# Four residual turns on a two-layer decoder trunk: where they stand on the load queue, and the order of the cases in the second column half of the down projection

## The chip, the cores and the metric

One Trainium2 chip, one of its cores. The time is device microseconds of one launch; three runs of the kernel before took 2044.64 to 2046.02 us, median 2045.53. Engines have short names: PE (matmul; PEld its weight loads), DVE (vector), ACT (scalar), POOL (GpSimd), SP (no arithmetic; here it issues nearly all DMAs, in program order).

## The reference, cut to what matters

A trunk of two layers over 256 tokens of width 2048, in float32: a mixer (gMLP gating in layer 0, latent attention in layer 1, each beside cross-attention into 256 memory tokens), then a gated ConvFFN. The change touches only the ConvFFN of both layers.

```python
def conv_ffn(h, w_up, cw, cb, w_down):     # h (256, 2048), w_up (2048, 11264), w_down (5632, 2048)
    a = h @ w_up
    ap = jnp.pad(a, ((0, 0), (CONV_W - 1, 0), (0, 0)))
    c = sum(ap[:, k:k + S] * cw[k] for k in range(CONV_W)) + cb
    gate, val = c[..., :D_FF], c[..., D_FF:]
    return (jax.nn.silu(gate) * val) @ w_down
...
x = x + conv_ffn(rmsnorm(x, g_ffn[l]), w_ffn_up[l], conv_w[l], conv_b[l], w_ffn_down[l])
```

## The kernel before

**Splitting.** Float32 products are made of three products of rounded halves. Each weight tile of 128 x 1024 floats (512 KB) is loaded into one of four tiles `raw`, ACT copies it rounded into `whi` (four tiles), DVE subtracts to get `wlo` (five tiles), and PE multiplies whi and wlo with the halves of the activations. A `raw` tile is free for the next load when DVE has made wlo; a `whi` tile is free when PE has used it. So loads run about four chunks ahead of the split and the split four ahead of PE. All weight loads go through SP's queue, which takes its entries in order: an entry that waits holds all behind it.

**Up projection.** 5632 columns are taken in 11 groups of 512, in three parts of 4, 4 and 3 groups. A group is two *passes* of PE (`gemm_fm`, L167): first gate, then value columns. A pass reads 2048 rows as eight *chunks* of 256 rows x 512 columns; each chunk is 24 matmuls (16 with whi, L161 and L162, and 8 with wlo, L164). Passes of a part are counted 0 to 7. Work that is to happen beside a pass hangs on it as `hooks`, a table from the chunk's number to functions that are called behind that chunk's matmuls. A pass's results go through DVE and ACT (convolution, SiLU, product).

**Turn.** The residual stream stands channel by channel (`x`, tile xT) and is needed token by token (`xt`) for the down projection. `turn(r)` (L1420), r from 0 to 3, makes one DVE transpose of 128 x 1024 floats into a tile `xs` (L1423) and four DMAs from xs to xt (L1427, 128 KB each in pieces of 32 floats). There are two tiles xs. All four turns hang on pass 3 of the first part, on chunks 0, 2, 4 and 6.

**Down projection.** A part of 4 groups has 2048 rows of `w_ffn_down`, eight *cases* k of 2 x 128 rows, and its output of 2048 columns is made in two *column halves* of 1024 (`down_phase`, L819), one after the other, with the cases in an order written in `FF_FAST`. A *plain* case splits its two row blocks and takes 24 matmuls of 512 columns. A *fast* case (k in 2, 3, 4, 5, 6) uses Winograd's form of a 2 x 2 block product and takes 21: it needs row block 1 (y), two tiles of block sums called t24 and t13, and the left half of row block 0 (x), split in this order (`fast_pair`, L800). The sums are four DVE adds of 128 x 512. They are made in one of three ways:

- *early* (`early_sums`, hung on the last passes), for the first column half;
- *stored* (`stored_sums`, L757): in a pass named in `FF_PASSES`, SP loads the two row blocks into the two tiles xs behind chunk 0, DVE adds (L759) behind chunk 3, POOL stores both tiles to DRAM (L785) behind chunk 5; the down projection loads them back (L861), into xs, or for case 5 of the second half into two `raw` tiles (`FF_RAW`);
- *late* (`late_sums`, L793): the down projection adds in place, from the loaded rows into xs.

With `FF_AHEAD`, the stored ones are case 3 of the first column half and cases 2, 5 and 4 of the second. In the second half cases 3 and 6 are late. Row tiles come from `raw`, for every third case from the two tiles `gate` (L851).

**What sets the order.** A scheduler places the instructions on each engine by its own timeline; inside `down_phase`, loads, splits and late sums are chained in the order in which they are written (`behind`).

Of the kernel before, what the change touches and what calls it, by code (L numbers as in the profile page):

```python
# [16 lines left out]
P = 128  # L17
# [15 lines left out]
FF_GROUPS = (4, 4, 3)  # L33
FF_EARLY = {4: (2, 6, 5), 3: (1, 2)}
FF_AHEAD = {4: ((3, 0), (2, 1), (5, 1), (4, 1)), 3: ()}
FF_PASSES = (0, 1, 2, 5), (1, 2, 4, 5), ()
FF_RAW = ((5, 1),)
FF_FAST = {
    4: (((2, 3, 4, 6, 5), (0, 1, 5, 2, 7, 3, 6, 4)), ((2, 3, 4, 6, 5), (0, 2, 1, 5, 3, 7, 4, 6))),
    3: (((1, 2, 4), (0, 3, 1, 5, 2, 4)), ((), (0, 1, 2, 3, 4, 5))),  # L40
}

# [35 lines left out]
class Kernel:  # L78
# [740 lines left out]
    def down_phase(self, dn, col, order, fast, lhs, rhs, pool, fp, between, evict, finish, late=0, late_gains=None, hooks={}, sums={}, stored={}):  # L819
        mm = self.nc.tensor.matmul  # L820
        names = ("m1", "m5", "m6", "m7"), ("e00", "e01", "e10", "e11")
        acc = {n: self.psum() for group in (names[::-1] if fast else names[1:]) for n in group}
        left, right = slice(0, 512), slice(512, 1024)
        todo = {n: 0 for n in acc}
        for k in order:
            for n in ("m1", "m5", "m6", "m7", "e00", "e01", "e10") if k in fast else names[1]:
                todo[n] += 1 if k in fast else 2
        total = dict(todo)

        def three(n, x, w, out=None, ends=None):  # L830
            (xh, xl), (wh, wl) = x, w
            start, stop = (todo[n] == total[n], todo[n] == 1) if ends is None else ends
            todo[n] -= 1
            o = acc[n] if out is None else out
            mm(o, xh, wh, start=start, stop=False)  # L835
            mm(o, xh, wl, start=False, stop=False)  # L836
            mm(o, xl, wh, start=False, stop=stop)  # L837

        def plain(k, ws, tb, half, **kw):
            cols = (left, right)[half]  # L840
            for i, (wh, wl) in enumerate(ws):
                three(f"e{tb}{half}", lhs(2 * k + i, tb), (wh[:, cols], wl[:, cols]), **kw)

        kept = []
        last_fast = [k for k in order if k in fast][-1:]
        for n, k in enumerate(order):
            raws = []
            for i in range(2):
                if n % 3 == (2 if col else 1) and n > 1:
                    raw = self.tmp(fp, [P, 1024], "gate", 2)  # L850
                else:  # L851
                    raw = self.wp.tile([P, 1024], F32, tag="raw", name=self.uid("raw"), bufs=4)
                c = 512 if (k in sums or (k, col // 1024) in stored) and i == 0 else 1024
                self.behind(self.nc.sync.dma_start(out=raw[:, :c], in_=dn[(2 * k + i) * P : (2 * k + i + 1) * P, col : col + c]))
                raws.append(raw)
            blocks = sums.get(k)
            if (k, col // 1024) in stored:
                tag, where, bufs = ("raw", self.wp, 4) if (k, col // 1024) in FF_RAW else ("xs", pool, 2)
                blocks = [self.tmp(where, [P, 1024], tag, bufs) for _ in range(2)]
                for i in (1, 0):  # L860
                    self.behind(self.nc.sync.dma_start(out=blocks[i], in_=stored[k, col // 1024][:, i]))  # L861
            elif k in fast and blocks is None:
                blocks = self.late_sums(raws, pool)
            if late_gains is not None and 2 <= n:
                late_gains(n - 2)
            if k in fast:
                names7 = "e00", "e01", "e10", "m6", "m5", "m7", "m1"
                for name, q, w in zip(names7, (1, 6, 2, 5, 4, 3, 0), self.fast_pair(raws, blocks)):
                    three(name, rhs(k, q), w)
                if k in last_fast:  # L870
                    between([acc[m] for m in names[0]])
            else:
                ws = self.plain_pair(raws)
                if n < len(order) - late:
                    for tb in range(2):
                        for half in range(2):
                            plain(k, ws, tb, half)
                else:
                    kept.append((k, ws))
            for f in hooks.get(n, ()):  # L880
                f()
        if not late:
            for tb in range(2):
                for half in range(2):
                    evict(tb, half, acc[f"e{tb}{half}"])
            return
        ET = mybir.EngineType
        with self.tc.manual_schedule(engines={ET.PE, ET.DVE, ET.Activation}):
            for half in range(2):
                for k, ws in kept:  # L890
                    plain(k, ws, 0, half)
                evict(0, half, acc[f"e0{half}"])
            for k, ws in kept:
                plain(k, ws, 1, 0)
            evict(1, 0, acc["e10"], meanwhile=lambda: finish(0))
            for k, ws in kept[:-1]:
                plain(k, ws, 1, 1)
            k, ws = kept[-1]
            e, rest = acc["e11"], self.psum()
            for i, (wh, wl) in enumerate(ws):  # L900
                three("e11", lhs(2 * k + i, 1), (wh[:, 512:768], wl[:, 512:768]), out=e[:, :256], ends=(False, i == 1))
            evict(1, 1, e, 0)
            for i, (wh, wl) in enumerate(ws):
                three("e11", lhs(2 * k + i, 1), (wh[:, 768:], wl[:, 768:]), out=rest[:, 256:], ends=(i == 0, i == 1))
            evict(1, 1, rest, 1)
            finish(1)


    def ffn(self, l, to_tokens, tokens):
# [6 lines left out]
        with self.tc.tile_pool(name=self.uid("ff"), bufs=1) as fp:  # L916
            g0 = 0
            for part, ng in enumerate(FF_GROUPS):
# [3 lines left out]
                fast = phases[0][0]  # L922
                parts7, o = {}, 0
                for k in fast:
                    n = 896 if k in phases[1][0] else 1024
# [22 lines left out]
                dn = down[g0 * 512 : (g0 + ng) * 512]  # L948
# [4 lines left out]
                for g in range(g0, g0 + ng):  # L953
# [34 lines left out]
                    hooks_g, hooks_v = dict(first) if g == 0 else {}, {}  # L988
                    if g == g0 + ng - 1:
                        hooks_g = sum_hooks  # L990
                    if g == 1:
                        hooks_v = to_tokens
                    if g == g0 + ng - 1:
                        hooks_v = ahead_hooks
                    if part and g == g0:
                        hooks_g = tokens.deferred()
                    both = lambda a, n: {i: a.get(i, []) + b.get(i, []) for b in (store_hooks.get(n, {}),) for i in {*a, *b}}
                    hooks_g, hooks_v = both(hooks_g, 2 * (g - g0)), both(hooks_v, 2 * (g - g0) + 1)
                    self.gemm_fm(self.rows(up, g * 512, 512), ks, 4, lambda k: xhl[k], eg, hooks=hooks_g)
                    self.gemm_fm(self.rows(up, FF + g * 512, 512), ks, 4, lambda k: xhl[k], ev, hooks=hooks_v)  # L1000
                g0 += ng
# [397 lines left out]
class Tokens:  # L1399
# [14 lines left out]
        return self.pool, 1024  # L1414

    def ffn(self, l):
        turns = {2 * r: [lambda r=r: self.turn(r)] for r in range(4)}
        self.k.ffn(l, turns, self)

    def turn(self, r):  # L1420
# [196 lines left out]
```

## Time and profile before

| | |
|---|---|
| median of 3 runs | 2045.53 us |
| profiled execution, its time | 2044.32 us |
| its span, first to last instruction | 2042.6 us |
| PE busy | 2019.6 us (99%) |
| DVE busy | 1650.9 us (81%) |
| ACT busy | 1177.1 us (58%) |
| PE's waits for ACT in up passes (L161 for L122) | 9.2 us in 5 |
| PE's waits for ACT in down projections (L835 for L713) | 3.1 us in 4 |
| granted TensorE clock, mean | 0.998 |

The span is shorter than the profiled execution's time by what lies around it. A row of a timeline is start, length, engine, line, operation, tiles written and read, and in brackets the idle time ahead and what ended it. Lines such as L835 (first product of a down case) are lines of the kernel before.

### The profile page before, as it was taken

What the parts mean: (1) busy time and instruction counts of PE and PEld (TensorE: products, weight loads), DVE (VectorE), ACT (ScalarE), POOL (GpSimd) and SP (SyncE); (2) the same over time, 40 slices, a digit from 0 to 9 for tenths busy, and PEclk for the clock granted to TensorE, in tenths of its full rate; (3) what the DMA queues carried; (4) which work ended last, traced back from release to release, by engine and by line L of the source; (5) the groups of instructions that cost most, each with busy time, mean ns of one, the idle gap of its engine ahead of it and who ended that gap; (6) DMA issues with size and microseconds to landing.
All of it is one profiled execution on the core that took longest, in us unless ns stands there. A gap on an engine that the chain in (4) does not pass through costs nothing.

```text
span 2042.6 us, 38329 instructions
## 1 busy us (share of the span) xinstructions
PE 2019.6 (99%) x15112; PEld 1909.2 (93%) x15112; DVE 1650.9 (81%) x2501; ACT 1177.1 (58%) x1687; POOL 130.0 (6%) x201
## 2 busy tenths in 40 slices
PE   9999999999999999999999999998999999999998
PEld 8989999999979999799989999998988999889996
DVE  6866767878988888887888786777898978888787
ACT  6754744545665556555566575444566555665555
POOL 0000013100000000000002141400000000000000
PEclk9999999999999999999999999999999999999999
DMA  8776556889668786677555634688876878667764
GB/s 253 234 216 183 165 194 210 272 213 308 217 222 277 250 305 209 221 216 229 178 194 183 185 113 160 207 260 220 305 225 223 290 241 305 205 222 218 236 203 148
DMA packets 262665, 455.40 MB, mean 223 GB/s; under 512 B 73102, under 2 KB 80596, under 8 KB 262484
## 3 DMA queue, kind: packets, MB, share of 16 engines
q1 hardware_dynamic: 257684, 435.63, 67.6%
q0 software_dynamic: 4608, 16.78, 2.3%
q8 instruction: 118, 1.93, 0.4%
q14 instruction: 63, 0.52, 0.1%
q10 hardware_dynamic: 192, 0.54, 0.1%
HBM read 429.82 MB, written 18.87 MB: 220 GB/s over the span
## 4 chain that ended last, share of the span: by engine, by line
PE 86%; DMA 5%; DVE 5%; ACT 2%; issue 1%; SPq 1%; ACTq 0%; DVEq 0%
PE ps L161 19%; PE ps L162 19%; PE ps L164 19%; PE ps L836 6%; PE ps L835 6%; PE ps L837 6%; PE ps L193 2%; PE ps L194 2%; PE ps L195 2%; DMA raw<-in_w_ffn_up 2%; DMA raw<-in_w_ffn_down 1%; PE ps L528 1%; DVE wlo L123 1%; DMA xs<-in_w_ffn_down 1%; DMA stored<-xs 1%
## 5 line engine op out<-in xcount | busy, mean ns | idle before, releaser
L122 ACT ACTIVATE whi<-raw 128x1024 fp32r<-128x1024 f32 x484 | 511.5, 1060 | 484.8 <-PE ps L162 303.9
L161 PE MATMUL ps<-xhl,whi 128*128 128x256 f32 x3264 | 765.0, 277 | 9.2 <-ACT whi L122 9.2
L123 DVE TENSOR_TENSOR wlo<-raw,whi 128x1024 fp32r<-128x1024 f32 x484 | 598.7, 1241 | 208.8 <-ACT whi L122 207.1
L162 PE MATMUL ps<-xhl,whi 128*128 128x256 f32 x3264 | 762.8, 276 | 0.0
L161 PEld LDWEIGHTS ps<-xhl,whi 128*128 128x128 f32 x3264 | 613.3, 188 | 10.9 <-ACT whi L122 10.2
L162 PEld LDWEIGHTS ps<-xhl,whi 128*128 128x128 f32 x3264 | 613.5, 188 | 0.7
L164 PE MATMUL ps<-xhl,wlo 128*128 128x256 f32 x3264 | 437.5, 276 | 0.2 <-DVE wlo L123 0.2
L164 PEld LDWEIGHTS ps<-xhl,wlo 128*128 128x128 f32 x3264 | 401.2, 188 | 0.4 <-DVE wlo L123 0.4
L836 PE MATMUL ps<-wlo,h 128*128 128x512 f32 x388 | 151.1, 390 | 0.0
L714 DVE TENSOR_TENSOR wlo<-raw,whi 128x1024 fp32r<-128x1024 f32 x100 | 120.8, 1220 | 31.8 <-ACT whi L713 31.0
L713 ACT ACTIVATE whi<-raw 128x1024 fp32r<-128x1024 f32 x100 | 104.7, 1056 | 69.1 <-PE ps L162 26.5
L943 ACT ACTIVATE c<-a,cT 128x256 f32<-128x256 f32 x176 | 99.6, 592 | 57.5 <-DVE a L241 57.1
L837 PE MATMUL ps<-whi,h 128*128 128x512 f32 x340 | 132.3, 390 | 0.0
L835 PE MATMUL ps<-whi,h 128*128 128x512 f32 x388 | 125.7, 394 | 3.6 <-ACT whi L713 3.1
L161 PE MATMUL ps<-mainhl,whi 128*128 128x256 f32 x512 | 119.7, 277 | 0.0
L162 PE MATMUL ps<-mainhl,whi 128*128 128x256 f32 x512 | 119.3, 276 | 0.0
L713 ACT ACTIVATE whi<-xs 128x1024 fp32r<-128x1024 f32 x60 | 62.1, 1057 | 60.1 <-DVE xs L793 26.3
L162 PEld LDWEIGHTS ps<-mainhl,whi 128*128 128x128 f32 x512 | 96.0, 188 | 0.0
L161 PEld LDWEIGHTS ps<-mainhl,whi 128*128 128x128 f32 x512 | 95.9, 188 | 0.0
L835 PEld LDWEIGHTS ps<-whi,h 128*128 128x128 f32 x388 | 71.8, 188 | 22.9 <-ACT whi L713 8.7
L128 DVE SCALAR_TENSOR_TENSOR wlo<-raw,gT,whi 128x512 fp32r<-128x512 f32 x96 | 71.5, 782 | 22.9 <-ACT whi L127 22.8
L714 DVE TENSOR_TENSOR wlo<-xs,whi 128x1024 fp32r<-128x1024 f32 x60 | 72.1, 1222 | 18.7 <-ACT whi L713 17.5
(388 smaller groups left out, 3032.1 us busy)
## 6 DMA issues: line engine op xcount, KB each, us to landing
raw<-in_w_ffn_up SPq DMA_DIRECT2D x352, 512.0 KB, 4.8
raw<-in_w_ffn_down SPq DMA_DIRECT2D x102, 512.0 KB, 5.5
raw<-in_w_out SPq DMA_DIRECT2D x64, 512.0 KB, 4.2
raw<-in_w_in_a SPq DMA_DIRECT2D x56, 512.0 KB, 4.5
gate<-in_w_ffn_down SPq DMA_DIRECT2D x42, 512.0 KB, 5.2
stored<-xs POOLq DMA_DIRECT2D x32, 512.0 KB, 5.2
raw<-in_w_mem_kv SPq DMA_DIRECT2D x31, 512.0 KB, 4.7
xs<-stored SPq DMA_DIRECT2D x24, 512.0 KB, 4.8
```

The source lines that it names most:

```text
L122: nc.scalar.activation(hi[:, :n], raw[:, :n], AF.Copy)
L123: nc.vector.tensor_tensor(lo[:, :n], raw[:, :n], hi[:, :n].bitcast(F32), ALU.subtract)
L128: nc.vector.scalar_tensor_tensor(lo[:, s], raw[:, s], gains[k], hi[:, s].bitcast(F32), ALU.mult, ALU.subtract)
L161: mm(acc[:, :S], wh, x[:, :S], start=first, stop=False)
L162: mm(acc[:, :S], wh, x[:, S:], start=False, stop=False)
L164: mm(acc[:, :S], wl, x[:, :S], start=False, stop=last)
L713: self.behind(self.nc.scalar.activation(hi, w, AF.Copy))
L714: self.behind(self.nc.vector.tensor_tensor(lo, w, hi.bitcast(F32), ALU.subtract))
L835: mm(o, xh, wh, start=start, stop=False)
L836: mm(o, xh, wl, start=False, stop=False)
L837: mm(o, xl, wh, start=False, stop=stop)
L943: nc.scalar.activation(c, a, AF.Identity, scale=w(2), bias=w(3))
```

## The change

All four parts of the edit are in the FFN.

1. `FF_PASSES`, first part: the pairs of stored sums hang on passes 2, 3, 4, 5 where they hung on 0, 1, 2, 5.
2. The turns: turns 0 and 1 hang on chunks 1 and 5 of pass 0, turns 2 and 3 on chunks 1 and 5 of pass 1, of the first group alone.
3. Second column half, parts of four groups: the order of cases is 0, 2, 1, 3, 5, 4, 7, 6 where it was 0, 2, 1, 5, 3, 7, 4, 6. Row tiles at place 5 come from `gate`: case 4's now, case 7's before.
4. A case with stored sums loads row block 1, t24, t13 and then the left half of row block 0, as they are used; before, it loaded the half row block 0, row block 1, t24, t13.

```diff
-FF_PASSES = (0, 1, 2, 5), (1, 2, 4, 5), ()
+FF_PASSES = (2, 3, 4, 5), (1, 2, 4, 5), ()
...
-    4: (((2, 3, 4, 6, 5), (0, 1, 5, 2, 7, 3, 6, 4)), ((2, 3, 4, 6, 5), (0, 2, 1, 5, 3, 7, 4, 6))),
+    4: (((2, 3, 4, 6, 5), (0, 1, 5, 2, 7, 3, 6, 4)), ((2, 3, 4, 6, 5), (0, 2, 1, 3, 5, 4, 7, 6))),
...
-                c = 512 if (k in sums or (k, col // 1024) in stored) and i == 0 else 1024
-                self.behind(self.nc.sync.dma_start(out=raw[:, :c], in_=dn[(2 * k + i) * P : (2 * k + i + 1) * P, col : col + c]))
                 raws.append(raw)
+            kept_sums = stored.get((k, col // 1024))
+            load = lambda o, a: self.behind(self.nc.sync.dma_start(out=o, in_=a))
+            row = lambda i, c: load(raws[i][:, :c], dn[(2 * k + i) * P : (2 * k + i + 1) * P, col : col + c])
             blocks = sums.get(k)
-            if (k, col // 1024) in stored:
+            if kept_sums is None:
+                row(0, 1024 if blocks is None else 512)
+                row(1, 1024)
+            else:
                 tag, where, bufs = ("raw", self.wp, 4) if (k, col // 1024) in FF_RAW else ("xs", pool, 2)
                 blocks = [self.tmp(where, [P, 1024], tag, bufs) for _ in range(2)]
+                row(1, 1024)
                 for i in (1, 0):
-                    self.behind(self.nc.sync.dma_start(out=blocks[i], in_=stored[k, col // 1024][:, i]))
-            elif k in fast and blocks is None:
+                    load(blocks[i], kept_sums[:, i])
+                row(0, 512)
+            if k in fast and blocks is None:
                 blocks = self.late_sums(raws, pool)
...
-                    if g == 1:
-                        hooks_v = to_tokens
...
-                    both = lambda a, n: {i: a.get(i, []) + b.get(i, []) for b in (store_hooks.get(n, {}),) for i in {*a, *b}}
-                    hooks_g, hooks_v = both(hooks_g, 2 * (g - g0)), both(hooks_v, 2 * (g - g0) + 1)
+                    if g == 0:
+                        hooks_g, hooks_v = hooks_g | to_tokens[0], to_tokens[1]
+                    hooks_g, hooks_v = store_hooks.get(2 * (g - g0), hooks_g), store_hooks.get(2 * (g - g0) + 1, hooks_v)
...
-        turns = {2 * r: [lambda r=r: self.turn(r)] for r in range(4)}
+        turns = [{1 + 4 * i: [lambda r=2 * n + i: self.turn(r)] for i in range(2)} for n in range(2)]
```

**SP's queue, layer 0, the four turns, before** (pass 3 of the first part). A row is the line, the operation, the tile written with its numbers and what is read; `xt<-xs` x4 is a turn, `raw<-in_w_ffn_up` a chunk's load.

```order
L1427 DMA xt_4187<-xs_709_5110 32x32x32 x4
L112 DMA raw_724_5248<-in_w_ffn_up 128x2x512
L112 DMA raw_727_5278<-in_w_ffn_up 128x2x512
L1427 DMA xt_4187<-xs_716_5176 32x32x32 x4
L112 DMA raw_731_5314<-in_w_ffn_up 128x2x512
L112 DMA raw_749_5389<-in_w_ffn_up 128x2x512
L1427 DMA xt_4187<-xs_723_5242 32x32x32 x4
L112 DMA raw_752_5419<-in_w_ffn_up 128x2x512
L112 DMA raw_755_5449<-in_w_ffn_up 128x2x512
L1427 DMA xt_4187<-xs_730_5308 32x32x32 x4
```

**The same turns in the change**: the first row stands behind the load of pass 0's last chunk; raw_626 is pass 1's first chunk, raw_665 pass 2's first.

```order
L1432 DMA xt_4187<-xs_590_4268 32x32x32 x4
L112 DMA raw_626_4503<-in_w_ffn_up 128x2x512
L112 DMA raw_629_4533<-in_w_ffn_up 128x2x512
L1432 DMA xt_4187<-xs_607_4405 32x32x32 x4
L112 DMA raw_633_4569<-in_w_ffn_up 128x2x512
L112 DMA raw_636_4599<-in_w_ffn_up 128x2x512
L112 DMA raw_639_4629<-in_w_ffn_up 128x2x512
L112 DMA raw_642_4659<-in_w_ffn_up 128x2x512
L1432 DMA xt_4187<-xs_632_4563 32x32x32 x4
L112 DMA raw_646_4695<-in_w_ffn_up 128x2x512
L112 DMA raw_649_4725<-in_w_ffn_up 128x2x512
L112 DMA raw_665_4796<-in_w_ffn_up 128x2x512
```

and directly behind them, where xs_668 and xs_669 are the first pair's tiles for stored sums, the same two places that turns 2 and 3 use:

```order
L764 DMA xs_668_4826<-in_w_ffn_down 128x1024
L112 DMA raw_670_4831<-in_w_ffn_up 128x2x512
L1432 DMA xt_4187<-xs_645_4689 32x32x32 x4
L112 DMA raw_673_4861<-in_w_ffn_up 128x2x512
L112 DMA raw_676_4891<-in_w_ffn_up 128x2x512
L764 DMA xs_669_4827<-in_w_ffn_down 128x512 x2
```

Two loads stand between the first two turns as before, four between the second and third and between the third and fourth; the first pair of stored sums stands on both sides of the fourth turn. On DVE the first transpose now stands at the start of the FFN:

```order
L255 SCALAR_TENSOR_TENSOR xhl_466_3354<-xT_81,gT_76,xhl_466_3354 128x256
L1428 STREAM_TRANSPOSE xs_590_4268<-xT_81 128x1024
L255 SCALAR_TENSOR_TENSOR xhl_466_3354<-xT_81,gT_76,xhl_466_3354 128x256 x3
L123 TENSOR_TENSOR wlo_603_4347<-raw_601_4345,whi_602_4346 128x1024
L123 TENSOR_TENSOR wlo_606_4377<-raw_604_4375,whi_605_4376 128x1024
L1428 STREAM_TRANSPOSE xs_607_4405<-xT_81 128x1024
```

These were four L255 in one row before; L255 makes operands for the last chunks of pass 0.

**SP's queue, layer 0, first part, second column half, before**: the two blocks of case 5, the rows of cases 3 and 7, the half row, row and blocks of case 4, and the rows of case 6.

```order
L861 DMA raw_1009_6996<-stored_687_4985 128x1024
L861 DMA raw_1008_6995<-stored_687_4985 128x1024
L854 DMA raw_1017_7035<-in_w_ffn_down 128x1024
L854 DMA raw_1018_7037<-in_w_ffn_down 128x1024
L854 DMA gate_1028_7081<-in_w_ffn_down 128x1024
L854 DMA gate_1029_7083<-in_w_ffn_down 128x1024
L854 DMA raw_1034_7117<-in_w_ffn_down 128x512
L854 DMA raw_1035_7119<-in_w_ffn_down 128x1024
L861 DMA xs_1037_7122<-stored_805_5850 128x1024
L861 DMA xs_1036_7121<-stored_805_5850 128x1024
L854 DMA raw_1045_7161<-in_w_ffn_down 128x1024
L854 DMA raw_1046_7163<-in_w_ffn_down 128x1024
```

**The same place in the change**, with the semaphores that each entry waits for: rows of case 3; row 1, t24, t13 and half row 0 of case 5; the same four of case 4; rows of case 7. Case 6's rows are the next two. A DMA signals one of eight DMAHW semaphores in turn, and waits for its own last use and for the load that last filled its tile; DMAHW3 is that of case 3's row block 1 (raw_1007), DMAHW2 that of its row block 0 (raw_1006), DMAHW7, ahead of this piece, that of case 2's row block 0.

```order
L855 DMA raw_1006_6991<-in_w_ffn_down 128x1024 [waits DMAHW2_49,DVE_49]
L855 DMA raw_1007_6992<-in_w_ffn_down 128x1024 [waits DMAHW3_49,DVE_49]
L855 DMA raw_1018_7038<-in_w_ffn_down 128x1024 [waits DMAHW4_49,DVE_49]
L855 DMA raw_1020_7040<-stored_766_5566 128x1024 [waits DMAHW7_49,DMAHW5_49,DVE_49]
L855 DMA raw_1019_7039<-stored_766_5566 128x1024 [waits DMAHW6_49,DMAHW3_49,DVE_49]
L855 DMA raw_1017_7037<-in_w_ffn_down 128x512 [waits DMAHW2_49,DVE_49]
L855 DMA gate_1029_7082<-in_w_ffn_down 128x1024 [waits DMAHW0_49]
L855 DMA xs_1031_7084<-stored_805_5850 128x1024 [waits DMAHW1_49]
L855 DMA xs_1030_7083<-stored_805_5850 128x1024
L855 DMA gate_1028_7081<-in_w_ffn_down 128x512
L855 DMA raw_1039_7125<-in_w_ffn_down 128x1024 [waits DMAHW4_49,DVE_49]
L855 DMA raw_1040_7126<-in_w_ffn_down 128x1024 [waits DMAHW5_49,DVE_49]
```

Case 3 came ahead of case 5, case 4 stands directly behind case 5, and case 7 between 4 and 6; the half row of each stored case went from first to last.

## The prediction

> **What bounds the kernel now.** I read the page first: PE is busy for 99% of the span, so only its stalls can be won. The waits of PE, first over the whole span, then by stretches (360 to 480, 1320 to 1440, 550 to 650, 840 to 900, 1800 to 1850 us), give their places; columns are total us, times, longest.
>
> ```profile
> PE 2019.6 (99%) x15112; PEld 1909.2 (93%) x15112; DVE 1650.9 (81%) x2501; ACT 1177.1 (58%) x1687; POOL 130.0 (6%) x201
> ...
> PE ps L161 <- ACT whi L122: 9.2, 5, 3.0
> PE ps L835 <- ACT whi L713: 3.1, 4, 1.5
> ...
> PE ps L161 <- ACT whi L122: 3.7, 2, 3.0
> PE ps L161 <- ACT whi L122: 5.4, 3, 2.8
> PE ps L835 <- ACT whi L713: 0.9, 1, 0.9
> PE ps L835 <- ACT whi L713: 1.9, 2, 1.5
> PE ps L835 <- ACT whi L713: 0.3, 1, 0.3
> ```
>
> All 9.2 us of L161 lie in two places, the fourth pass of each layer's FFN, where the four turns stand. The L835 waits lie in second column halves. What is late in the fourth pass, by SP's timeline and then ACT's and PE's:
>
> ```profile
> 417.23 5.08 SPq L1427 DMA_DIRECT2D xt<-xs  x4
> 422.41 1.47 SPq L112 DMA_DIRECT2D raw<-in_w_ffn_up  x2
> ...
> 431.77 6.62 SPq L1427 DMA_DIRECT2D xt<-xs  x4
> 438.49 1.89 SPq L112 DMA_DIRECT2D raw<-in_w_ffn_up  x2
> 440.47 5.29 SPq L1427 DMA_DIRECT2D xt<-xs  x4
> 445.85 12.73 SPq L112 DMA_DIRECT2D raw<-in_w_ffn_up  x6
> ...
> 452.50 1.06 ACT L122 ACTIVATE whi<-raw 128x1024 fp32r<-128x1024 f32 x1 [5.56 <-DMA raw<-in_w_ffn_up]
> ...
> 453.61 0.39 PE L161 MATMUL ps<-xhl,whi 128*128 128x256 f32 x1 [3.00 <-ACT whi L122]
> ```
>
> Each turn holds the queue for 5.1 to 6.6 us, and only two weight loads get between two turns. From the first turn to the load at 445.85 that is 28.6 us for six loads. PE eats a chunk (24 matmuls) in 2.72 us, eight of them at 0.91 us by the chain row below, so it needed ten and a half. The load lands at 452.4, ACT splits it in 1.06, PE stands.
>
> ```profile
> 363.86 0.91 PE ps L164 x8
> 598.91 1.13 PE ps L835 x5
> ...
> 363.00:373.00 10.00, 10.00 (x88) 9.95 (x87) 8.00 (x10) 5.32 (x6) 0.00 (x0) 1.00 0.74 250
> 454.00:464.00 10.00, 10.00 (x76) 10.00 (x76) 10.00 (x20) 6.06 (x9) 0.00 (x0) 0.83 0.66 206
> ```
>
> The windows (length, busy us of PE, PEld, DVE, ACT, POOL, then the granted clock, DMA share, GB/s) show one more price: behind the 3.00 us stall the clock is 0.83 for 10 us, so 1.7 us are lost with PE "busy". Layer 1's stalls, 2.8 us at most, have no such row. The Trainium skill (TensorE: Matmul & The Clock Gate, What's actually happening) lets the clock fall to half only after an idle window of about 3.4 us, whose phase runs freely. By its length the 3.00 us stall would be too short and the term 0 instead of 1.7. The row decides, and the sum keeps 1.7.
>
> **The change part by part.**
>
> *Turns.* Sixteen issues per layer leave the fourth pass, with four DVE transposes of 1.24 us; two turns go into each pass of the first group. Removed if none of it returns: 3.7 + 5.4 us of waits and 1.7 us of clock, 10.8. Idle counts too late: a 256-column matmul is 0.28 us long in the row below, and the next starts 0.11 after it, so each stall holds 0.17 more, five times 0.17 = 0.8. Together 11.6 us.
>
> Does it return? The start of layer 0's FFN:
>
> ```profile
> 353.73 0.28 PE L161 MATMUL ps<-xhl,whi 128*128 128x256 f32 x1
> 353.84 0.28 PE L162 MATMUL ps<-xhl,whi 128*128 128x256 f32 x1
> ...
> 353.25 1.42 DVE L667 TENSOR_TENSOR xT<-ps,xT 128x256 f32<-128x256 f32 x4 [0.36 <-PE ps L164]
> 354.58 1.44 DVE L123 TENSOR_TENSOR wlo<-raw,whi 128x1024 fp32r<-128x1024 f32 x1
> 355.94 3.36 DVE L255 SCALAR_TENSOR_TENSOR xhl<-xT,gT,xhl 128x256 fp32r<-128x256 f32 x4
> ...
> L1423 DVE STREAM_TRANSPOSE xs<-xT 128x1024 f32<-128x1024 f32 x4 | 5.0, 1240 | 2.0 <-DMA xt<-xs 2.0
> L759 DVE TENSOR_TENSOR xs<-xs,xs 128x512 f32<-128x512 f32 x8 | 5.5, 688 | 3.1 <-DMA xs<-in_w_ffn_down 3.0
> ...
> xt<-xs SPq DMA_DIRECT2D x32, 128.0 KB, 6.3
> raw<-in_w_ffn_up SPq DMA_DIRECT2D x352, 512.0 KB, 4.8
> ```
>
> In the new order the first transpose stands behind one L255, so it ends near 356.8 + 1.24 = 358.1. The first turn's issues take 5.1 to 6.6 and end at 363.2 to 364.7; two loads follow at the pace of their split, then the second turn, to 370 to 373. The load behind it is pass 1's third chunk. Landing 4.8 (median) to 6.6 us later (the 445.85 load) and 1.06 for ACT give 376.1 to 380.9. PE starts at 353.7, so pass 1 at 353.7 + 8 x 2.72 = 375.5 and that chunk at 380.9. Slack 0 to 5 us. Four loads then pass before the third turn. The fourth turn is the other narrow place: behind it only two loads are ahead of xs_669, which needs that turn's landing (6.3 us), and SP waits. That turn's transpose stands behind the split of pass 1's sixth chunk, whose split tile PE frees with the second chunk, at 375.5 + 2 x 2.72 = 380.9; with the split (1.1 on ACT, 1.2 on DVE) and the transpose it is near 385, its issues end near 391, its pieces land near 397. Then xs_669 goes, and at 397.6 the next load, pass 2's fifth chunk, split by 397.6 + 5.5 + 1.1 = 404.2; PE wants it at 375.5 + 21.8 + 10.9 = 408.2. Slack 4. I take 0.5 us of new stall per layer, 0 to 5.5 as bounds (5.5 is layer 1's whole old cost), so 11.6 - 1.0 = 10.6.
>
> *Stored sums into passes 2 to 5.* Two pairs per layer move from passes 0 and 1: four adds of 0.69 and 1 MB in, 1 MB out each. Pass 3 loses 5.0 us of transposes and gains 2.7 of adds; the total on DVE and DMA is unchanged. What covers it, in windows of an old pass with a pair (397), with turns (419) and with a pair again (461):
>
> ```profile
> 397.00:419.00 22.00, 22.00 (x196) 22.00 (x195) 18.70 (x32) 11.58 (x17) 1.06 (x2) 1.00 0.89 296
> 419.00:441.00 22.00, 22.00 (x196) 22.00 (x195) 16.59 (x23) 9.70 (x14) 0.00 (x0) 1.00 0.92 183
> 461.00:483.00 22.00, 22.00 (x196) 22.00 (x195) 21.90 (x37) 13.20 (x18) 1.06 (x2) 1.00 0.91 301
> ```
>
> A pair runs beside a full PE. Cost 0, but DVE has 0.1 us left in the last of them; without this cover see the third rival.
>
> *Second halves, four of them per kernel.* The old stall before the last case, 6 (SP, then ACT, then PE):
>
> ```profile
> 597.11 1.46 SPq L861 DMA_DIRECT2D xs<-stored  x2
> 598.67 0.85 SPq L854 DMA_DIRECT2D raw<-in_w_ffn_down  x2
> ...
> 607.34 1.06 ACT L713 ACTIVATE whi<-raw 128x1024 fp32r<-128x1024 f32 x1 [0.95 <-DMA raw<-in_w_ffn_down]
> 610.97 2.01 ACT L713 ACTIVATE whi<-xs 128x1024 fp32r<-128x1024 f32 x2 [2.57 <-DVE xs L793]
> ...
> 612.08 0.73 PE L835 MATMUL ps<-whi,h 128*128 128x512 f32 x2 [0.93 <-ACT whi L713]
> ```
>
> Case 6's rows stand behind case 4's two blocks; the second, issued near 599.1, lands 8.1 us later, then four adds, then ACT, and PE waits 0.93. In the new order a plain case, 7, stands between 4 and 6. A matmul of 512 columns takes 0.227 us (1.13 for five), so a fast case 21 x 0.227 = 4.8 and a plain one 24 x 0.227 = 5.4. Case 6's rows now wait for case 5's tiles, freed one by one up to near 598, so they no longer leave as one burst, and its sums start when 7's splits are done, near 604.3; 604.3 + 2.7 + 1.1 = 608.1 against PE's 610.7. The old waits go: 3.1 + 4 x 0.16 (0.39 long, 0.227 apart) = 3.7 us.
>
> What is late next: case 5's blocks. They lie in raw tiles; the semaphores in the rows of the change show t24 in the tile of case 2's row 0, free at 581.5 as before, and t13 in the tile of case 3's row 1, free once case 1's split (583.30 + 1.23 below), the sums (2.7) and that row's split are done: 588.5. With 5.5 us for landing and 1.1 for ACT it is there at 595.1; PE, at 590.5 with case 3, wants it 29 matmuls later, at 597.1. Only then, behind case 3's row 0 at 591.5, do case 4's four loads leave, 1.75 MB close together with case 5's half row. With 6.5 us they are split 0.4 us before PE wants t24 of case 4 (600.5); with 8.1, 1.2 us too late. I take 0.3 per half, 0 to 1.2 as bounds: 3.7 - 1.2 = 2.5.
>
> ```profile
> 583.30 1.23 DVE L714 TENSOR_TENSOR wlo<-gate,whi 128x1024 fp32r<-128x1024 f32 x1 [0.37 <-ACT whi L713]
> ...
> raw<-in_w_ffn_down SPq DMA_DIRECT2D x102, 512.0 KB, 5.5
> ```
>
> *First halves.* Only the stored case 3 changes, its half row asked for last. PE shows no wait there; it is read last on PE too. Cost 0.
>
> Sum on the profiled span: 2042.6 - 10.6 - 2.5 = 2029.5. That execution took 2044.32, 1.7 beyond its span and 1.2 under the median of 2045.53, so as a median 2045.5 - 13.1 = **2032.4 us**.
>
> **The rivals.**
>
> *The turns' stall only moves.* For it: a turn's time is its small pieces, 92% DMA share at 183 GB/s in the 419 window against 89% at 296, and a slack of 0 at the slow end. Against: two turns a pass rather than four, and the two in front start with all loads ahead. Then only the clock and the second halves are won: 2045.5 - 1.7 - 2.5 = 2041.3. The Trainium skill (DMA: Bandwidth & Descriptors, Specifications) wants 512 bytes at least for line rate; the turn's pieces are 32 floats, 128 bytes. The rule speaks for this rival, since moving a turn makes no piece larger.
>
> *Second halves get worse.* If 8.1 us is the landing time of each burst, 1.2 us a half in t24 and about as much again in t13 behind it: 4 x 2.4 = 9.6 instead of 3.7 gone: 2045.5 - 10.6 - 3.7 + 9.6 = 2040.8; with half of it, 2036.
>
> *DVE becomes the bound, slower than before.* DVE works in order and stands at an add until its block lands: 3.1 us before eight adds (L759 row). In passes 2 to 5 it now meets four pairs in a row with 0.1 us spare. ACT and the loads are about 11 us ahead of PE (four split tiles of 2.72 us). If each pair costs DVE more than (11 + 8)/4 = 4.8 us of standing, a layer loses over 8 us, and two lose more than the 15 saved; at 5.5 us it is 2 x (22 - 11) = 22, so 2045.5 - 13.1 + 22 = 2054. Against: three pairs in a row ran in passes 0 to 2 without a PE wait.
>
> **How the numbers follow.** Forecast, both stalls mostly gone (2027 to 2036): 0.65. Second halves worse: 0.15. Turn stall moved: 0.11. DVE bound: 0.05. Another place, either sign: 0.04. If no stall replaces the old ones, 2045.5 - 15.3 = 2030; a few tenths of unlisted short waits put the low end at 2027. Upwards the range takes in the second rival: 2041. A measurement of this kernel tells about 0.2% (4 us) from no change: faster 0.86 (the forecast, the second rival, part of the first), same 0.08, slower 0.06.
>
> **What would show it.** Right: no wait of PE on L122 in the fourth pass of either layer, clock 1.00 behind it; turns in pairs on SP with four loads before the third; none or under 0.5 us of L835 waits in second halves. Wrong: PE waits in the second or third pass (third chunk, fifth chunk), a wait for case 4's or 5's blocks, or DVE at 22 of 22 with idle time "<-DMA xs" in passes 2 to 5.

## The result

The changed kernel took 2027.24 us (median of 5, 2025.17 to 2030.53) beside 2044.64 for the kernel before: a ratio of 0.9921, 95% interval 0.9906 to 0.9935, so 17.4 us less. A second comparison on another chip gave 0.9924 (0.9903 to 0.9944), 2027.65 beside 2042.88, so 15.2 us less; one of its four executions, at 2523.7 us, is left out of the ratio. The forecast was 2032.4, in a range of 2027 to 2036. Ahead of the second comparison, 12 to 15 us were expected if the two halves of the edit (below) simply add up and 16 to 19 if each makes room for the other; its interval, 11.4 to 19.8 us, decides nothing between them.

The page's engine line and the full list of PE's waits of the changed kernel, the span being 2023.5 us:

```profile
PE 2013.4 (100%) x15112; PEld 1907.3 (94%) x15112; DVE 1649.4 (82%) x2501; ACT 1181.3 (58%) x1687; POOL 128.2 (6%) x201
...
PE ps L495 <- DVE ones L292: 1.1, 1, 1.1
PE ps L836 <- DVE wlo L714: 0.2, 1, 0.2
PE ps L608 <- DVE pT L250: 0.2, 1, 0.2
```

Both groups of the prediction, L161 for L122 and L835 for L713, are gone, and what is left lies outside the change. SP's timeline shows the turns (L1432 now) in pairs with four loads before the third, and the windows (the columns as before) a full PE at clock 1.00 in the first two passes and where the stall with the slow clock had been:

```profile
358.30 4.12 SPq L1432 DMA_DIRECT2D xt<-xs  x4
362.51 1.50 SPq L112 DMA_DIRECT2D raw<-in_w_ffn_up  x2
364.22 5.97 SPq L1432 DMA_DIRECT2D xt<-xs  x4
370.30 2.86 SPq L112 DMA_DIRECT2D raw<-in_w_ffn_up  x4
373.78 7.37 SPq L1432 DMA_DIRECT2D xt<-xs  x4
...
353.00:375.00 22.00, 22.00 (x195) 21.95 (x194) 19.64 (x23) 10.74 (x13) 6.75 (x8) 1.00 0.79 186
375.00:397.00 22.00, 22.00 (x197) 22.00 (x196) 15.28 (x21) 12.98 (x17) 0.00 (x0) 1.00 0.96 243
440.00:465.00 25.00, 25.00 (x223) 25.00 (x222) 21.21 (x36) 12.26 (x14) 1.06 (x2) 1.00 0.80 276
```

In the second half, ACT's rows for case 5's two blocks, then case 4's first block:

```profile
586.58 1.07 ACT L713 ACTIVATE whi<-raw 128x1024 fp32r<-128x1024 f32 x1 [0.70 <-PE ps L837]
587.94 1.06 ACT L713 ACTIVATE whi<-raw 128x1024 fp32r<-128x1024 f32 x1 [0.29 <-PE ps L837]
...
593.38 1.06 ACT L713 ACTIVATE whi<-xs 128x1024 fp32r<-128x1024 f32 x1 [0.72 <-DMA xs<-stored]
```

Case 5's blocks lie ready and ACT waits for PE; ACT waits 0.7 us for case 4's first block, and it still comes in time for PE.

**A measure by stretches.** The waits of a list leave out the short ones and what the clock costs, so I measure PE's late time otherwise. All kernels here have 15112 matmuls, and the start of the same numbered matmul marks the same piece of work. The first part of layer 0's up projection runs from the first matmul below to the second, before and after:

```profile
353.73 0.28 PE L161 MATMUL ps<-xhl,whi 128*128 128x256 f32 x1
534.24 0.40 PE L835 MATMUL ps<-whi,hhx 128*128 128x512 f32 x1
```

```profile
353.88 0.28 PE L161 MATMUL ps<-xhl,whi 128*128 128x256 f32 x1
528.42 0.40 PE L835 MATMUL ps<-whi,hhx 128*128 128x512 f32 x1
```

That is 180.5 and 174.5 us. Over all fourteen traces, only six stretches vary by more than 0.05 us once the start, which takes 352.1 to 354.6 us, is past: the two first up parts (shortest 174.55) and the four down projections of four groups, each with some matmuls on either side (shortest 94.49, 95.58, 93.67, 94.80). The time above the shortest, added over the two up parts and over the four down projections, is "late up" and "late down" below, in us. An execution's time less its late up and late down is 2024.5 to 2025.9 us in thirteen of the fourteen, and 2027.0 in the one that started latest, so these stretches hold nearly all that differs between the kernels. The experiments ran in three groups on three chips; the kernel before had medians of 2042.3, 2042.9 and 2042.2 there, single executions from 2035.6 to 2054.9.

| kernel | median us (runs) | ratio to before, 95% | late up | late down |
|---|---|---|---|---|
| before | see above | 1 | 12.8 | 6.5 |
| before, second profile | 2043.4 (1) | | 8.7 | 8.9 |
| changed | 2027.2 (5) | 0.9906 to 0.9935 | 0.0 | 0.1 |
| changed, second profile | 2027.7 (4) | 0.9903 to 0.9944 | 1.3 | 1.5 |
| turns and sums alone | 2035.4 (12) | 0.9951 to 0.9979 | 4.8 | 8.9 |
| second halves alone | 2036.2 (12) | 0.9949 to 0.9979 | 7.0 | 2.7 |
| turns, sums, order of cases | 2033.3 (7) | 0.9947 to 0.9978 | 0.0 | 8.4 |
| turns, sums, order of loads | 2035.9 (9) | 0.9957 to 0.9983 | 0.0 | 10.1 |
| turns issued by POOL | 2038.0 (1) | | 5.2 | 7.4 |
| turns in 2 KB pieces | 2038.4 (1) | | 1.9 | 9.5 |
| changed, sums on 0, 1, 2, 5 | 2038.1 (10) | 0.9954 to 0.9997 | 11.5 | 2.2 |
| changed, four turns in one pass | 2046.5 (1) | | 17.4 | 4.4 |
| the same again | 2035.4 (10) | 0.9958 to 0.9981 | 4.9 | 5.4 |
| changed, pairs 10 chunks apart | 2029.1 (4) | 0.9914 to 0.9943 | 0.0 | 3.1 |

Late up and late down are of one profiled execution each, and one kernel's size differs from one to the next. Kernels with the old place of turns and sums show 12.8, 8.7 and 7.0 us of late up (the third is the second halves alone). The old down projection shows 6.5 to 9.5 us of late down in five profiles, the new one 0.1 to 5.4 in seven.

### The profile page after: what moved, and what is told of

Same layout as the page of the kernel before. It is cut to its first block, busy times and chain, and to the rows that moved or that the text cites. A ratio compares the mean times of both kernels' runs of the same rounds, so it can differ in the third digit from the quotient of the medians.

```text
span 2023.5 us, 38369 instructions
## 1 busy us (share of the span) xinstructions
PE 2013.4 (100%) x15112; PEld 1907.3 (94%) x15112; DVE 1649.4 (82%) x2501; ACT 1181.3 (58%) x1687; POOL 128.2 (6%) x201
## 4 chain that ended last, share of the span: by engine, by line
PE 99%; DVE 0%; ACT 0%; issue 0%; ACTq 0%
PE ps L161 22%; PE ps L162 22%; PE ps L164 22%; PE ps L835 7%; PE ps L836 7%; PE ps L837 7%; PE ps L193 2%; PE ps L194 2%; PE ps L195 2%; PE ps L528 1%; PE ps L410 0%; PE ps L608 0%; PE ps L607 0%; PE ps L606 0%; PE ps L1300 0%; PE ps L1088 0%
## 5 line engine op out<-in xcount | busy, mean ns | idle before, releaser
L122 ACT ACTIVATE whi<-raw 128x1024 fp32r<-128x1024 f32 x484 | 512.5, 1061 | 490.5 <-PE ps L162 321.9
L161 PE MATMUL ps<-xhl,whi 128*128 128x256 f32 x3264 | 763.3, 277 | 0.0
L161 PEld LDWEIGHTS ps<-xhl,whi 128*128 128x128 f32 x3264 | 612.7, 188 | 0.4
L713 ACT ACTIVATE whi<-raw 128x1024 fp32r<-128x1024 f32 x104 | 109.0, 1056 | 60.1 <-PE ps L162 29.1
L835 PE MATMUL ps<-whi,h 128*128 128x512 f32 x388 | 122.2, 391 | 0.0
L161 PE MATMUL ps<-mainhl,whi 128*128 128x256 f32 x512 | 119.6, 277 | 0.0
L161 PEld LDWEIGHTS ps<-mainhl,whi 128*128 128x128 f32 x512 | 95.9, 188 | 0.0
L713 ACT ACTIVATE whi<-xs 128x1024 fp32r<-128x1024 f32 x60 | 62.3, 1058 | 53.2 <-DVE xs L793 26.1
L835 PEld LDWEIGHTS ps<-whi,h 128*128 128x128 f32 x388 | 72.4, 188 | 16.4 <-ACT whi L713 1.7
L836 PEld LDWEIGHTS ps<-wlo,h 128*128 128x128 f32 x388 | 72.8, 188 | 15.0
```

The costliest lines, as they stand in the source:

```text
L122: nc.scalar.activation(hi[:, :n], raw[:, :n], AF.Copy)
L161: mm(acc[:, :S], wh, x[:, :S], start=first, stop=False)
L713: self.behind(self.nc.scalar.activation(hi, w, AF.Copy))
```

## The experiments

### The two halves of the edit apart

One kernel has the turns and sums of the change with the old down projection, the other the reverse.

> The kernel before with the up projection's part of the edit alone: the turns on chunks 1 and 5 of the first group's two passes, the stored sums on passes 2 to 5; order of cases and loads of the down projection as before. Theory A (each turn holds the load queue for 5 to 7 us, and with two loads between turns the chunks came late; spread out, the loads ahead of the split cover it): PE's waits of 9.2 us on L122 go, the waits on L713 of about 3 us in the second column halves stay; the matmuls' own late starts show 12.7 us gone with the waits and their clock, so about 2044.6 - 12.7 = 2032. Rival B (the stall of the turns only moves, and the gain came from the second halves): 2041 or more. Rival C (the two parts need each other): between, 2034 to 2041.

> The kernel before with the down projection's part of the edit alone: new order of cases in the second column halves and blocks loaded as used; turns and stored sums as before. Theory A (the two parts add up): the waits of 9.2 us on L122 stay, the waits on L713 in the second halves go; by the term of the prediction 3.7 us, by the late starts of matmuls in both traces about 6 us: 2038.5 to 2041. Rival C (the parts need each other): no gain, 2044 to 2046.

PE's waits, the turns alone first, then the second halves alone:

```profile
PE ps L835 <- ACT whi L713: 6.3, 7, 1.5
PE ps L161 <- ACT whi L122: 2.5, 2, 2.2
```

```profile
PE ps L161 <- ACT whi L122: 4.5, 2, 3.1
PE ps L835 <- ACT whi L713: 1.5, 4, 0.6
```

The medians fall by 6.9 and 6.1 us, 13.0 together: each half gains alone, so neither rival B of the first nor rival C of the second holds. The 2035.4 of the turns alone lies in the range given for rival C there, and whether the two parts also help each other stays open. The turns alone won less than theory A's 12.7, for two reasons. The old stall is not always 12.8 us (8.7 and 7.0 in two other profiles). And this profiled execution, the slowest of its twelve, has a stall that no step of mine named, in layer 1 at 1436. SP, then ACT and PE:

```profile
1419.23 2.35 SPq L112 DMA_DIRECT2D raw<-in_w_ffn_up  x2
1428.93 0.81 SPq L764 DMA_DIRECT2D xs<-in_w_ffn_down  x2
...
1435.23 1.06 ACT L122 ACTIVATE whi<-raw 128x1024 fp32r<-128x1024 f32 x1 [1.93 <-DMA raw<-in_w_ffn_up]
...
1436.34 0.39 PE L161 MATMUL ps<-xhl,whi 128*128 128x256 f32 x1 [2.19 <-ACT whi L122]
```

From 1421.6 to 1428.9 SP stands at a pair's load, whose tile xs the store of the pair before has not yet left; the chunk loads behind it are late. SP's waits of this kind, first part of layer 1, turns alone and then the changed kernel:

```profile
SPq L764 <- DMA stored<-xs: 25.1, 6, 7.3
```

```profile
SPq L764 <- DMA stored<-xs: 20.7, 6, 4.2
```

The second halves alone gave 6.1, where the forecast had 2.5 (3.7 gross).

### Who issues the turns, and in which pieces

In the kernel before, the sixteen transfers of a layer's turns go to another queue, or keep queue and place and move the same bytes in longer pieces. The second kernel leaves out the order of the values in xt that the down projection needs, so it is a probe of the transfers and no candidate.

```diff
-            nc.sync.dma_start(out=o[:, q], in_=xs[32 * q : 32 * (q + 1)].rearrange("j a k i -> j (a k) i"))
+            nc.gpsimd.dma_start(out=o[:, q], in_=xs[32 * q : 32 * (q + 1)].rearrange("j a k i -> j (a k) i"))
```

> The kernel before with one change: the sixteen transfers of the turns in each layer are issued by POOL (GpSimd) instead of SP. Their bytes, pieces, place in the fourth pass and transposes stay. Theory A (the load queue is held while SP issues the small pieces, and that alone is why chunks came late): the waits of PE on L122 in the fourth pass go, about 12 us less, 2032 to 2034. Rival B (the small pieces fill the 16 DMA engines, whoever issues them; the loads behind them land late): the waits stay, 2042 to 2045.

```diff
-        o = self.xt[32 * r : 32 * (r + 1)].rearrange("j a (k q i) -> j q (a k) i", q=4, i=32)
+        o = self.xt[32 * r : 32 * (r + 1)].rearrange("j a (q n) -> j a q n", q=4)
...
-            nc.sync.dma_start(out=o[:, q], in_=xs[32 * q : 32 * (q + 1)].rearrange("j a k i -> j (a k) i"))
+            nc.sync.dma_start(out=o[:, :, q], in_=xs[32 * q : 32 * (q + 1)].rearrange("j a k i -> j a (k i)"))
```

> The kernel before with one change: each transfer of a turn moves the same 128 KB from and to the same tiles from the same queue at the same place, but in contiguous pieces of 512 floats (2 KB) instead of 32 floats (128 bytes). What changes in the computation is the arrangement of the residual's values in xt. Theories A and B both rest on the size of the pieces: SP would be held well under 2 us a turn, the DMA share in the fourth pass would fall from 0.92 and PE's waits on L122 would go, 2032 to 2034. Rival D (the pieces do not matter; the transposes on DVE or the wait for a tile xs at four turns in one pass made the chunks late): the waits stay at about 9 us, 2043 to 2045.

With POOL's queue (a row each of POOL and DVE, then PE's two waits):

```profile
425.32 0.79 POOL L1427 DMA_DIRECT2D xt<-xs  x1 [4.62 <-issue]
...
433.33 1.25 DVE L1423 STREAM_TRANSPOSE xs<-xT 128x1024 f32<-128x1024 f32 x1 [6.08 <-issue]
...
PE ps L164 <- DVE wlo L123: 2.3, 2, 1.4
PE ps L161 <- ACT whi L122: 1.7, 1, 1.7
```

SP now has loads alone in these passes, and the DMA share from 419 to 441 is 0.92 as before, yet 5.2 us of the 7.0 to 12.8 stay. The first turn's fourth transfer leaves POOL only at 425.3 and lands at 433.2. The third transpose needs that turn's tile, DVE stands 6.1 us ahead of it, and splits stand behind it. So the hold of the load queue is not the only way in which the turns make chunks late, and neither theory holds alone. How much of the stall it was is not shown: this is one execution, 1.8 us below the smallest old stall.

With 2 KB pieces (SP's rows, the window, PE's wait):

```profile
418.54 3.03 SPq L1427 DMA_DIRECT2D xt<-xs  x4
...
428.94 4.74 SPq L1427 DMA_DIRECT2D xt<-xs  x4
...
419.00:441.00 22.00, 22.00 (x197) 22.00 (x196) 17.69 (x25) 11.10 (x16) 0.00 (x0) 1.00 1.03 243
...
PE ps L161 <- ACT whi L122: 1.1, 2, 0.9
```

Late up falls to 1.9 with everything else in place, transposes and tiles included: rival D falls, by this one execution. But my own numbers were off too: SP is still held 3.0 to 4.7 us a turn here (2.5 to 5.3 in layer 1), and the DMA share rises to 1.03. The window moves more, 243 GB/s where the old kernel's moved 183. The total of 2038.4 is one execution with 9.5 us late down, which the edit doesn't touch.

### Where the turns and the sums may stand

```diff
-FF_PASSES = (2, 3, 4, 5), (1, 2, 4, 5), ()
+FF_PASSES = (0, 1, 2, 5), (1, 2, 4, 5), ()
```

> The changed kernel, but with the four stored pairs on passes 0, 1, 2 and 5, where they hung before, so that turns and pairs share the passes 0 and 1 and their two tiles xs. Theory A (moving the turns is what counts, the place of the pairs is free): within 2 us of the changed kernel. Rival E (pairs and turns in the same pass wait for each other's tiles xs, SP stands at such an entry with the chunk loads behind it): PE waits for L122 return in passes 0 to 3, 3 to 8 us a layer, so 6 to 16 us above the changed kernel.

The median is 10.4 us above that of the changed kernel, in rival E's range. One of its two stalls, by rows of SP, DVE, ACT and PE:

```profile
416.50 6.71 SPq L1433 DMA_DIRECT2D xt<-xs  x4
423.31 0.65 SPq L764 DMA_DIRECT2D xs<-in_w_ffn_down  x1
...
428.34 0.69 DVE L759 TENSOR_TENSOR xs<-xs 128x512 f32<-128x512 f32 x1 [2.75 <-DMA xs<-in_w_ffn_down]
...
429.40 1.09 ACT L949 ACTIVATE c<-a,cT 128x256 f32<-128x256 f32 x2 [5.07 <-DVE a L241]
...
431.49 0.39 PE L161 MATMUL ps<-xhl,whi 128*128 128x256 f32 x1 [4.09 <-ACT whi L122]
```

The turns, which wait for the pairs' tiles xs, now leave at 380.7 to 416.5, where the changed kernel's first leaves at 358.3, and a pair's load stands behind the fourth. The chunk that PE wants at 427.4 leaves SP only at 424.0, behind both, and lands at 429.9; so most of the 4.1 us is the load queue's, as in the kernel before. DVE at the add and ACT behind DVE hold the chunk's split from 429.9 to 430.4, half a us more.

```diff
-        turns = [{1 + 4 * i: [lambda r=2 * n + i: self.turn(r)] for i in range(2)} for n in range(2)]
+        turns = [{2 * r: [lambda r=r: self.turn(r)] for r in range(4)}, {}]
```

> The changed kernel, but with all four turns on the first pass (chunks 0, 2, 4 and 6); pairs on passes 2 to 5 as in the change. Theory A (what stalls PE is the spacing: sixteen small-piece transfers with only two loads between the second and the third turn): PE waits for L122 come back in the second pass, 2 to 5 us a layer, 4 to 10 us above the changed kernel. Rival H (it is the place that counts: at the start of the FFN the lead of the loads covers four turns too): no such wait, within 2 us of it.

> All four turns on the first pass, once more, timed in rounds. Its first execution took 2046.5: 10.6 us more of late matmul starts than the changed kernel, and about 9 us from matmuls that started 120 ns apart where 113 is the rule, for some 155 us behind a stall of 2.6 us, at a granted clock of 1.00. Theory A (the stalls behind the turns come each time; the slow pitch is one of the things that can follow a stall, not each time): a spread of times, most of them 2035 to 2040, some 2046. Rival J (the slow pitch belongs to this program): all near 2046.

SP in layer 0, in the first of the two profiled executions:

```profile
357.86 7.81 SPq L1432 DMA_DIRECT2D xt<-xs  x8
365.77 1.44 SPq L112 DMA_DIRECT2D raw<-in_w_ffn_up  x2
367.33 10.38 SPq L1432 DMA_DIRECT2D xt<-xs  x8
```

Two loads in 20 us, and PE stalls 2.4 us up to 383.7 in one execution and 2.8 up to 385.2 in the other. The ten executions of the second run (2030.9 to 2040.6) have a median 7.7 us above that of the changed kernel (on another chip, before alike), within the 4 to 10 of theory A: a start with loads ahead isn't enough, and rival H falls. The 2046.5 did not come again, so rival J falls too, but theory A's spread was only partly right: four of the ten lie between 2035 and 2040, five below, and none near 2046. What the 2046.5 held is in the last section.

```diff
-FF_PASSES = (2, 3, 4, 5), (1, 2, 4, 5), ()
+FF_CHUNKS = (16, 26, 36, 46), (8, 20, 32, 42), ()
```

> The changed kernel, but with the pairs of stored sums 10 chunks apart in the first part (from chunk 0 of the third pass) and 10 or 12 apart in the second part, where they are 8 apart in adjacent passes. Theory F (in the change SP stands at a pair's load until the store of the pair before has landed, 17.1 and 20.7 us in the two layers' first parts, and in some executions that makes chunks late: 2.2 us of PE in the run with the turns alone): these waits of SP fall below 10 us a layer, PE has no wait for L122, the slow end of the times goes: 0 to 2 us below the median of the changed kernel. Rival G (the loads' lead covers the hold in nearly all executions): no difference over 1 us in the median.

```profile
SPq L764 <- DMA stored<-xs: 9.1, 3, 3.9
...
SPq L764 <- DMA stored<-xs: 8.6, 3, 3.5
```

SP's waits for stores halve, as expected (first parts of layers 0 and 1), but the median doesn't fall: 2029.1 against 2027.7, with overlapping intervals, and no late up in either layer. Theory F's gain is not there, and rival G fits better, though 1.4 us is a little over its bound. The hold is real, but in most executions the loads' lead covers it. No kernel here beats the changed one.

### The order of cases and the order of loads

Each goes alone on top of the turns and sums (the diff of the change shows both).

> The kernel with the turns and sums of the change (the first experiment) plus the new order of cases in the second column halves; the blocks are loaded in the old order. Theory A (the order of cases carries the second halves' gain: a plain case between 4 and 6 gives case 6's sums time): about 5 to 6 us below the run with turns and sums alone, so 13 us below before, and no L713 wait over 1 us before case 6. Rival I (the order of loads carries it): within 2 us of turns and sums alone, 7 below before.

> The kernel with the turns and sums of the change plus the new order of loads (row block 1, both blocks of sums, then the half row); the old order of cases. Theory A: case 6 still stands behind case 4's blocks, the L713 waits of 1 to 1.5 us stay, within 2 us of turns and sums alone (7 below before). Rival I: about 13 below before, no such wait.

The medians are 2033.3 and 2035.9, beside 2035.4 with the old down projection (another chip, before alike), while both together gave 2027.2 and 2027.7. With the new loads alone, theory A's forecast came: 6.3 us below before, and the old waits stay. With the new order alone it failed: 8.9 below, not 13. So neither carries the gain alone. The new order of cases with old loads (SP, then ACT at case 5's second block and case 4's row block 1, then PE):

```profile
582.37 3.46 SPq L861 DMA_DIRECT2D raw<-stored  x2
...
590.02 1.06 ACT L713 ACTIVATE whi<-raw 128x1024 fp32r<-128x1024 f32 x1 [2.62 <-DMA raw<-stored]
...
593.41 1.06 ACT L713 ACTIVATE whi<-gate 128x1024 fp32r<-128x1024 f32 x1 [1.81 <-DMA gate<-in_w_ffn_down]
...
594.52 0.73 PE L835 MATMUL ps<-whi,h 128*128 128x512 f32 x2 [0.48 <-ACT whi L713]
```

In the changed kernel these two loads go at 576.86 and 583.42 where they go at 582.37 and 585.50 here, since case 5's half row no longer goes ahead of them and takes a `raw` tile:

```profile
576.86 6.89 SPq L855 DMA_DIRECT2D raw<-stored  x2
```

With the old loads, ACT stands at case 5's second block, whose load left late, and then at case 4's row block 1, which lands at 593.4, 7.0 us after it leaves; in the changed kernel it lands at 591.6, in 4.7 us. The listed waits of PE in the second halves all lie in case 4. So the order of cases moves the stall from case 6 to case 4, and the order of loads lifts that one. The old order of cases with new loads keeps the old stall at case 6, whose rows still leave in a burst behind case 4's blocks, and adds to the one at case 3's sums: waits of up to 1.3 us, where the first profile of the kernel before has 0.4 at most:

```profile
602.84 1.06 ACT L713 ACTIVATE whi<-raw 128x1024 fp32r<-128x1024 f32 x1 [2.71 <-DMA raw<-in_w_ffn_down]
...
PE ps L835 <- ACT whi L713: 7.2, 8, 1.3
```

### The kernel before, a second time

> The kernel before, profiled a second time. Theory A (the stalls' size differs from execution to execution, so that one profiled execution does not size the gain): the waits for L122 lie in the same fourth passes and those for L713 in the same second halves, with totals that differ from 9.2 and 3.1 us by 1 us or more. Rival K (the stalls are the same each time): 9.2 and 3.1 within 0.5 us.

```profile
PE ps L835 <- ACT whi L713: 6.2, 7, 1.6
PE ps L161 <- ACT whi L122: 6.1, 3, 3.7
```

Same places, other sizes: 6.2 us where it was 3.1, 6.1 where it was 9.2, as theory A says. The sum of late time is 17.6 us against 19.3.

## Why the prediction was right, and where its sum was short

**The mechanism held.** Both stalls went, by the steps named, and no rival came true. The medians fell 17.4 and 15.2 us where the sum had 13.1; in the two profiled executions the span fell 19.1 us, late up and late down 19.2 (12.8 and 6.4). The time lies at the very low end of the range. That end, 2027, is 3 us below the 2030 that the prediction worked out without new stalls, and "a few tenths of unlisted short waits" do not make 3 us. In the profiled execution the old stalls held some 4 us more than the 15.3 of the sum, so that the range reached that far is partly luck.

**Mis-sized: the second halves, "3.7 us" gross.** It came from the waits listed (3.1) plus 0.16 for each. That same execution lost 6.5 us in these stretches. Four waits at case 3's and case 6's sums, of 0.08 to 0.14 us and too short for the list, each made a matmul 0.24 to 0.30 us late, and behind all eight the matmul after that started another 0.11 late. A second profile lost 8.9. The edit alone was worth 6.1 in the median.

**Mis-sized: the residuals, "0.5 us of new stall per layer" and "0.3 per half".** Late up and late down are 0.0 and 0.1 us in one profile of the changed kernel, 1.3 and 1.5 in the other, against 1.0 and 1.2. The down term came where it was named: with the new down projection PE stands at case 4's t24, 0.6 us at most in the second profile. It can be larger than the term: five other profiles with the same down projection have 2.2 to 5.4 us, most of it in case 4. The up term came at neither of the two narrow places named. At the first, the fast end of the bounds decided: the first turn's issues took 4.1 us, not 5.1 to 6.6, and the second's ended at 370.2, in the range 370 to 373. The later turns held the queue longer than the sum took, up to 7.4 us (9.5 in the second profile), but the transfers landed in 3.6 us in the median, not 6.3, and at the second place xs_669 and the load behind it left at 396.1 and 397.0, where the prediction has 397 and 397.6.

**Mis-sized, the other way at times: the turns, "11.6 us".** Late up was 12.8 us in the profile it was read from, 8.7 in the next, and 7.0 with the second halves alone.

**"Cost 0" for the moved sums** held in the changed kernel to within 1.3 us, but not always: four pairs in adjacent passes make SP stand for stores about twice as long as before, and the profiled run with the turns alone lost 4.8 us in layer 1. The 1.3 us also stand behind such a hold, of 6.1 us; that it alone is their cause is not shown. The term also leaves out that the sums had to move: left in place, they cost 10.4.

**Case 5's and case 4's blocks.** Case 5's were split by 589.0; the prediction's 595.1 less the 5.8 us by which this down projection began earlier is 589.3. That these agree is partly luck: t13's load left at 583.42, 0.7 us later than worked out, landed in time, and ACT waited for PE, not for the block. Case 4's t24 was split at 594.4, in time, and in the second profile PE waited 0.6 and 0.2 us for it, a small case of what was named as a sign of being wrong. The step was right, and the experiment with old loads shows these two cases to be the narrow place.

**The rivals.** *The stall only moves* is what a closer spacing gives: four turns in one pass brought it back. *Second halves get worse* named the place where late down is left, but it stays below the old 6.5 to 9.5 us. *DVE becomes the bound* did not come; its mechanism, DVE standing at an add with the rest behind it, shows in the run with the sums left in place, where it added half a us to a stall of 4.1. The Trainium skill (DMA: Bandwidth & Descriptors, Specifications) wants pieces of 512 bytes at least for line rate. The trace agrees: with 2 KB pieces in the old place the window moved 243 GB/s, not 183, and late up was 1.9 us. But the change got rid of the stall with pieces of 128 bytes, so longer pieces are one cure and not the only one.

## What to carry to other kernels

What small-piece transfers on a load queue cost depends on how closely they stand. Compare the time they hold the queue with the lead of the loads, and count every other transfer and tile that has to pass them. When a stall is moved, list what is late next and look whether a second edit already covers it; here the order of cases was worth little without the order of loads, and the turns' new place nothing like as much without moving the sums. And size a gain from the length of a stretch of work between two fixed instructions, in more than one execution, not from the listed waits of one.

## What the runs showed of the hardware that was not expected

**A stall can be followed by a slower matmul pitch.** In the first execution with four turns in one pass, behind a stall of 2.64 us that ended at 1346.8, matmuls of 256 columns started 120 ns apart where 113 is the rule elsewhere, until the up part ended near 1502. The granted clock was 1.00 there, except in the first 3.4 us. Windows, this run and then the second profile of the changed kernel:

```profile
1380.00:1400.00 20.00, 20.00 (x169) 20.00 (x168) 16.61 (x27) 10.74 (x16) 1.06 (x2) 1.00 0.83 274
```

```profile
1380.00:1400.00 20.00, 20.00 (x179) 20.00 (x178) 14.45 (x21) 10.61 (x15) 1.07 (x2) 1.00 0.83 291
```

169 matmuls against 179, some 9 us in all. No other profile has it outside its first or last 20 us; its cause is open, and no profile shows whether it lies behind the longest execution of the kernel before, 2054.9 us, too.

**The clock falls by how much PE idles in one stretch of a fixed grid, not by the stall's length.** Away from the two ends of the traces the granted clock fell eight times in these fourteen profiles, each time to 0.50 for 3.41 us. Two falls of one profile, or a fall and the one at the profile's end, begin a whole multiple of 3.413 us apart. Each came behind a stretch of that grid in which PE idled 2.1 to 3.3 us; the most idle stretch without a fall behind it had 1.7. The shortest stall with a fall, the 2.19 us of the turns alone (columns as before):

```profile
1434.22:1437.64 3.42, 1.30 (x11) 1.30 (x12) 1.53 (x3) 2.41 (x4) 0.00 (x0) 1.00 1.02 384
1437.64:1441.05 3.41, 3.41 (x19) 3.41 (x18) 3.41 (x7) 1.53 (x2) 0.08 (x1) 0.50 0.57 181
```

A stall of 2.83 us in the kernel before cost no clock, as it lay across two stretches with 1.1 and 1.7 us. So the prediction's 1.7 us of clock (half of 3.41) comes or stays away by where a stall falls on the grid. Four turns in one pass show the difference in layer 0: late up was 4.3 us there with a stall of 2.4 us and a fall, 3.1 us in the other execution with a stall of 2.8 us and none. The Trainium skill (TensorE: Matmul & The Clock Gate, What's actually happening) lets the clock fall after an idle window of about 3.4 us; the length agrees with the grid here, but 2.1 us idle in a window were enough.

**Longer pieces do not free the DMA engines.** In the window of the turns they raised what was moved from 183 to 243 GB/s and the DMA share from 0.92 to 1.03, and the turns' transfers themselves landed later, 9.1 us in the median against 6.3.
